# Projections of the delta rule's heads 4 to 7 as nested block products

## The chip, the cores and the metric

The kernel runs on one core of a Trainium2 chip. A core has five engines with a queue of instructions each, worked off in order: TensorE (PE: matmuls, with PEld for loading its stationary operand), VectorE (DVE), ScalarE (ACT), GpSimd (POOL) and SyncE (SP), which here issues the DMAs. They meet through semaphores. Operands lie in SBUF (128 partitions), matmul results in PSUM banks of 128 x 512 floats, everything else in DRAM. The metric is device time in microseconds (us) of one execution.

## The reference, cut to what matters

The kernel computes a layer of 1024 tokens and model width 1024: a feed-forward, a mixer, a second feed-forward, each added to the running x. All is float32.

```python
x = x + 0.5 * swiglu(rms_norm(x), ffn1...)          # gate and up 1024 -> 2816, down 2816 -> 1024
h = rms_norm(x)
proj = h @ w_in                                      # q,k,v | z | b | a | ssm z | ssm x,B,C | dt
q, k, v = silu(causal_dwconv(proj[qkv]))             # 8 heads of 128 channels, 4 taps
o = gated_delta_rule(l2_normalize(q), l2_normalize(k), v, g, beta)
o = rms_norm(o) * silu(proj[z])
y = ssd_scan(...)                                    # 16 state-space heads
x = x + concat([o, y]) @ w_out
x = x + 0.5 * swiglu(rms_norm(x), ffn2...)

# delta rule, chunk by chunk, state S (128 x 128) of each head:
t_inv = inverse(eye + strict_lower(beta * (k @ k.T) * decay))
v_new = t_inv @ (beta * v) - (t_inv @ (beta * exp(gc) * k)) @ S
o     = (q * exp(gc)) @ S + (q @ k.T * decay) @ v_new
S     = S * g_tot + (k * exp(gc_end - gc)).T @ v_new
```

## The kernel before

Every float32 matmul is made of three in a rounded format: both operands are split into a high part (a cast) and a low part (the rest), and hi x hi, lo x hi and hi x lo are summed in one PSUM bank (`mm3`, L120 to 123). Weights are split by `wsplit` (L125 to 138), ScalarE casting (L136) and VectorE subtracting (L137), or by `split2` (L238 to 243). One matmul covers 128 x 128 weights and 512 tokens.

The stages follow one another: first feed-forward (gate and up, then Down), projections and scan of the state-space part (four units), the delta rule (eight heads), the output projection, the second feed-forward.

The feed-forwards and the output use nested block products: a product of matrices cut into 2 x 2 blocks is made of seven block products in place of eight, whose operands are sums and differences of blocks. `a_ops` (L304) makes the weight operands of gate and up on VectorE (sums L315) and ScalarE and VectorE (split, L239 and L240), `prod` (L328) multiplies one. `gate_up_all` calls its inner `prep` (L427) between products, `Down` (L494) has a `prep` (L519) as well; these prepare what later products need.

The input projection is plain. `w_seq` lists the column blocks of w_in, `next_w` hands one out, already split, and prefetches the next into the tile `wst`, with its parts in `whi` and `wlo`. `proj_half` (L757) multiplies 128 columns with 512 tokens of the normalized tokens (`hhi`, `hlo`): 8 blocks x 3 = 24 matmuls, so q, k, v and z of one head take 8 x 24 = 192.

One head of the delta rule (L1112 to 1308):

- q, k, v, z are projected; `conv_silu` (L773) copies the projection into `pre` on ScalarE, multiplies one tap there, and adds three on VectorE (L784). `zc` is the gate, stored to DRAM (L1126).
- k k and q k products of the eight token blocks (L1149, L1150), from which `u` is made.
- The unit lower triangles are inverted. 32 x 32 pieces of `u` go through DRAM (`fs_u`, L1169) and come back as `fu` (L1196), one piece on each partition. Forward substitution takes 31 steps of two VectorE operations, each dependent on the one before it (`ft` L1206, `fx` L1208). The result goes through DRAM again (`fs_x`, L1211, four stores) and comes back by eight small copies into `lv` and `u` (L1218, L1219), all on SP's queue; VectorE transposes `lv` (L1220).
- The solve: small matmuls (L1226 to 1252) put the pieces together, between them copies of ScalarE and VectorE. `kd`, the decayed keys, is scaled out of transposes (L1263, L1265).
- The recurrence over eight blocks (L1269 to 1297), a chain through TensorE and VectorE: k S (L1275), `rr` (L1277), u rr (L1280), `vn` (L1282), k vn (L1289), the new state `sn` (L1294); the output of a block into `vr` by ScalarE (L1297).
- `vr` is normalized (L1303 squares, L1307) and stored to mix_scr.

Work of neighbouring heads overlaps: the substitution of head h runs beside the recurrence of head h - 1, and the projections of head h + 1 fill TensorE between their steps. A scheduler sets each engine's order when the program is built; the queues then run in that order, whatever the times turn out to be. Heads are numbered from 0.

With the last head, `out_start` (L1101) begins the output projection: `group_prep(0)` (L1092) loads rows of w_out into `wst` and makes `mtt` from the state-space outputs. `mtt` lies where hhi and hlo lay.

## Time and profile before

| what | us |
|---|---|
| median of three runs | 2308.49 (2307.07 to 2310.89) |
| the profiled execution, its own time | 2309.97 |
| its span in the trace | 2308.2 |
| TensorE busy | 2272.5 |
| VectorE busy | 1725.1 |
| ScalarE busy | 1088.8 |
| DMA, both ways | 281.42 MB, 122 GB/s on average |

The profile's page gives busy time by engine, the chain of work that ended last, and groups of instructions by line; windows of the trace give the same by stage. A row of a group is: line, engine, operation, written tile <- read tile, shape, count | busy time, mean ns of one | idle time of the engine ahead of it and what ended it. A row of the timeline begins with the start and the duration in us. Matmuls overlap, so that the distance of two starts and not the duration says what one costs. The granted clock is TensorE's, 1.00 at full speed.

### The profile page before, as it was taken

To read this page: it belongs to the slowest core of one execution; us is meant where nothing else is said; L and a number is where in the kernel's file an instruction comes from. 1 tells how busy PE (TensorE), PEld (TensorE's weight loads), DVE (VectorE), ACT (ScalarE), POOL (GpSimd) and SP (SyncE) were. 2 spreads that over 40 slices of the span, in tenths; PEclk is the share of its full clock that TensorE was granted. 3 is DMA by queue.
4 is the path that set the end of the run, shared out by engine and by line. 5 is a ranking of instruction groups with operands and counts; after the bars stand their busy time and mean duration, and the time that the engine had idled before them with its cause. 6 is when DMAs were issued, how large, how long until landed. Compare 5 with 4: busy or idle time off the path is not lost.

```text
span 2308.2 us, 31393 instructions
## 1 busy us (share of the span) xinstructions
PE 2272.5 (98%) x11750; PEld 1858.9 (81%) x11750; DVE 1725.1 (75%) x3349; ACT 1088.8 (47%) x1884; POOL 53.1 (2%) x125
## 2 busy tenths in 40 slices
PE   7999999999999999999999999999999999999998
PEld 5788888888878888878788888788778888888886
DVE  7977776767765675668777888878688777766787
ACT  7433333343367785863555555332543333334344
POOL 0000000000000100000000000000000000000000
PEclk9999999999999999999999999999999999999999
DMA  3333332573652332232333322335223333329446
GB/s 111 127 114 102 105 109 97 178 278 128 222 179 78 92 92 81 67 85 74 83 101 83 82 74 73 104 110 193 79 84 117 109 103 105 109 88 354 139 154 214
DMA packets 231438, 281.42 MB, mean 122 GB/s; under 512 B 57449, under 2 KB 164045, under 8 KB 230261
## 3 DMA queue, kind: packets, MB, share of 16 engines
q1 hardware_dynamic: 231028, 279.31, 37.5%
q8 instruction: 92, 1.51, 0.3%
q14 instruction: 62, 0.50, 0.1%
q0 software_dynamic: 256, 0.10, 0.0%
HBM read 211.59 MB, written 67.77 MB: 121 GB/s over the span
## 4 chain that ended last, share of the span: by engine, by line
PE 87%; DVE 6%; ACT 3%; DMA 2%; issue 1%; SPq 0%; POOL 0%; DVEq 0%; ACTq 0%
PE ps_pj L121 9%; PE ps_pj L123 9%; PE ps_pj L122 9%; PE ps_pj L334 6%; PE ps_pj L332 6%; PE ps_pj L333 6%; PE ps_mx L332 3%; PE ps_mx L334 3%; PE ps_mx L333 3%; PE ps_pj L553 2%; PE ps_pj L554 2%; PE ps_pj L552 2%; PE ps_oo L333 2%; PE ps_oo L332 2%; PE ps_oo L334 2%; PE ps_sc L552 1%
## 5 line engine op out<-in xcount | busy, mean ns | idle before, releaser
L121 PE MATMUL ps_pj<-hhi,whi 128*128 128x512 f32 x832 | 334.3, 402 | 0.4 <-ACT gsb L826 0.4
L123 PE MATMUL ps_pj<-hhi,wlo 128*128 128x512 f32 x832 | 334.5, 402 | 0.0
L122 PE MATMUL ps_pj<-hlo,whi 128*128 128x512 f32 x832 | 331.8, 399 | 0.0
L334 PE MATMUL ps_pj<-bh,al 128*128 128x512 f32 x688 | 267.9, 389 | 0.0
L333 PE MATMUL ps_pj<-bl,ah 128*128 128x512 f32 x688 | 267.8, 389 | 0.0
L332 PE MATMUL ps_pj<-bh,ah 128*128 128x512 f32 x688 | 267.6, 390 | 0.0
L123 PEld LDWEIGHTS ps_pj<-hhi,wlo 128*128 128x128 f32 x832 | 156.7, 188 | 29.6 <-issue 1.9
L122 PEld LDWEIGHTS ps_pj<-hlo,whi 128*128 128x128 f32 x832 | 156.7, 188 | 29.1 <-issue 1.2
L121 PEld LDWEIGHTS ps_pj<-hhi,whi 128*128 128x128 f32 x832 | 156.8, 188 | 28.8 <-ACT gsb L826 0.9
L239 ACT CAST ah<-wst 128x512 fp32r<-128x512 f32 x88 | 54.6, 623 | 223.8 <-PE ps_oo L333 131.4
L239 ACT CAST hid<-hraw 128x1024 fp32r<-128x1024 f32 (+1 forms) x84 | 82.3, 981 | 147.9 <-PE ps_oo L554 62.5
L333 PEld LDWEIGHTS ps_pj<-bl,ah 128*128 128x128 f32 x688 | 129.2, 188 | 26.8
L334 PEld LDWEIGHTS ps_pj<-bh,al 128*128 128x128 f32 x688 | 129.1, 188 | 26.7
L332 PEld LDWEIGHTS ps_pj<-bh,ah 128*128 128x128 f32 x688 | 128.9, 188 | 26.5
L315 DVE TENSOR_TENSOR as<-wst 128x512 f32<-128x512 f32 x220 | 144.8, 683 | 3.3 <-DMA wst<-in_ffn_w_up_dram 3.1
L240 DVE TENSOR_TENSOR al<-as,ah 128x512 fp32r<-128x512 f32 x220 | 140.9, 684 | 4.8 <-ACT ah L239 4.0
L332 PE MATMUL ps_mx<-bh,ah 128*128 128x512 f32 x352 | 138.3, 395 | 4.0 <-ACT m L341 1.4
L333 PE MATMUL ps_mx<-bl,ah 128*128 128x512 f32 x352 | 138.3, 393 | 0.5 <-DVE bl L240 0.5
L334 PE MATMUL ps_mx<-bh,al 128*128 128x512 f32 x352 | 137.7, 391 | 0.3 <-DVE al L240 0.3
L239 ACT CAST ah<-as 128x512 fp32r<-128x512 f32 x220 | 125.0, 618 | 22.6 <-DVE as L315 22.6
L240 DVE TENSOR_TENSOR hid<-hraw,hid 128x1024 fp32r<-128x1024 f32 (+1 forms) x84 | 95.0, 1131 | 34.8 <-ACT hid L239 34.3
L341 ACT COPY m<-ps_pj 128x512 f32<-128x512 f32 x88 | 51.6, 588 | 124.5 <-PE ps_pj L334 122.3
(448 smaller groups left out, 5085.0 us busy)
## 6 DMA issues: line engine op xcount, KB each, us to landing
hraw<-hid_scr SPq DMA_DIRECT2D x70, 512.0 KB, 3.9
hid_scr<-hs SPq DMA_DIRECT2D x110, 256.0 KB, 2.3
wst<-in_ffn_w_down_dram SPq DMA_DIRECT2D x50, 512.0 KB, 4.7
wst<-in_ffn_w_gate_dram SPq DMA_DIRECT2D x22, 1024.0 KB, 5.6
wst<-in_ffn_w_up_dram SPq DMA_DIRECT2D x22, 1024.0 KB, 5.4
wst<-in_w_in_dram SPq DMA_DIRECT2D x36, 512.0 KB, 4.8
hid_scr<-sg SPq DMA_DIRECT2D x44, 256.0 KB, 2.0
keep<-in_ffn_w_down_dram SPq DMA_DIRECT2D x20, 512.0 KB, 5.5
```

The costliest lines, as they stand in the source:

```text
L121: T.matmul(o, lhsT=wh, rhs=mh, start=first, stop=False)
L122: T.matmul(o, lhsT=wh, rhs=ml, start=False, stop=False)
L123: T.matmul(o, lhsT=wl, rhs=mh, start=False, stop=last)
L239: return (A.copy(out=hi, in_=src), V.tensor_tensor(out=lo, in0=src, in1=hi.bitcast(F32), op=ALU.subtract))
L240: V.tensor_tensor(out=lo, in0=src, in1=hi.bitcast(F32), op=ALU.subtract))
L315: V.tensor_tensor(out=t, in0=v[0], in1=v[1], op=v[2])
L332: T.matmul(bank, lhsT=wh[:, k], rhs=bh[:, k], start=a, stop=False, skip_group_check=True)
L333: T.matmul(bank, lhsT=wh[:, k], rhs=bl[:, k], start=False, stop=False, skip_group_check=True)
L334: T.matmul(bank, lhsT=wl[:, k], rhs=bh[:, k], start=False, stop=z, skip_group_check=True)
L341: A.copy(out=t, in_=bank)
L552: T.matmul(bank, lhsT=hh, rhs=wh, start=first and k == 0, stop=False, skip_group_check=True)
L553: T.matmul(bank, lhsT=hh, rhs=wl, start=False, stop=False, skip_group_check=True)
```

## The change

Heads 4 to 7 project q with k, and v with z, by `chunk`: the two column blocks by the two halves of the inner dimension, times the two halves of the inner dimension by the two halves of the tokens. Seven block products of 12 matmuls replace eight of 12. Their weight operands (units) are made during the first feed-forward by `win_units` (six chunks beside gate and up, two beside Down) and stored to DRAM, 7 units of 512 KB for each of 8 chunks; in the delta rule `unit_load` brings them back into four slots, which lie in the tiles of `wst`. The token operands of four of the products are made during the state-space stage by `token_operands`, stored, and loaded once before head 4: three pairs into `natp`'s, `whi`'s and `wlo`'s tiles and into halves of hhi and hlo. In all heads `kd`, `vn` and the scaling of `vr` move from VectorE to ScalarE. `conv_from` takes its first tap from SBUF. `zc` and `qsq` share a tile.

```diff
@@ gate_up_all's prep
+                for _ in range(2 if i % 8 == 7 else 1):
+                    next(side, None)
@@ Down.prep
+            if self.cnt % 2:
+                next(self.side, None)
@@
-    for h in range(GH):
+    for h in range(4):
         w_seq.append((COL_Q + h * P, COL_K + h * P))
         w_seq.append((COL_V + h * P, COL_GZ + h * P))
@@ win_units, for each chunk c
+            raw = raws.tile([P, 2, NK, P], F32, name="wraw")
+            for j, c0 in enumerate(((COL_Q, COL_K), (COL_V, COL_GZ))[c % 2]):
+                nc.sync.dma_start(out=raw[:, j], in_=win_v[:, :, c0 + (c // 2 + NESTED) * P:c0 + (c // 2 + NESTED + 1) * P])
...
+            def unit(m, src):
+                parts = [raws.part(dt) for dt in (F32R, F32R)]
+                split(*parts, src)
+                for i, t in enumerate(parts):
+                    nc.sync.dma_start(out=wu_scr[c][:, IN_ORDER.index(m), i], in_=t.bitcast(F32))
...
+            yield
+            unit(4, a22)
+            s1 = summed(a21, a22, ALU.add)
+            yield
+            unit(5, s1)
...
@@ state-space loop
         proj_z(zts)
+        token_operands(un)
@@
+    def unit_load(s):
+        if s < 7 * len(wu_scr):
+            c, i = divmod(s, 7)
+            u = slots[s % 4]
+            nc.sync.dma_start(out=u.bitcast(F32), in_=wu_scr[c][:, i])
+            units.append((s, u))
+
+    def unit_prod(bank, m, first):
+        s, u = units.pop(0)
+        bh, bl = H_IN[m]
+        for k in range(4):
+            wh, wl = (u[:, i, k * P:(k + 1) * P] for i in range(2))
+            T.matmul(bank, lhsT=wh, rhs=bh[k], start=first and k == 0, stop=False, skip_group_check=True)
+            T.matmul(bank, lhsT=wh, rhs=bl[k], start=False, stop=False, skip_group_check=True)
+            T.matmul(bank, lhsT=wl, rhs=bh[k], start=False, stop=k == 3, skip_group_check=True)
+        unit_load(s + 4)
+
+    def chunk(d0, d1):
+        lo, hi = slice(0, 512), slice(512, L)
+        x = psum("pj")
+        unit_prod(x, 1, True)
+        A.copy(out=d1[:, lo], in_=x)
+        y = psum("pj")
+        unit_prod(y, 6, True)
+        V.tensor_tensor(out=y, in0=y, in1=d1[:, lo], op=ALU.add)
+        A.copy(out=d0[:, hi], in_=y)
+        unit_prod(x, 2, False)
+        A.copy(out=d0[:, lo], in_=x)
+        unit_prod(y, 7, False)
+        z = psum("pj")
+        unit_prod(z, 5, True)
+        A.copy(out=d1[:, hi], in_=z)
+        V.tensor_tensor(out=d1[:, hi], in0=y, in1=d1[:, hi], op=ALU.add)
+        unit_prod(z, 3, False)
+        V.tensor_tensor(out=d0[:, hi], in0=z, in1=d0[:, hi], op=ALU.add)
+        unit_prod(y, 4, False)
+        A.copy(out=d1[:, lo], in_=y)
+
+    def conv_from(pre, c, dst):
+        A.mul(out=dst, in_=pre[:, 3:3 + L], mul=cw_g[:, 3, c:c + 1])
+        conv_taps(pre, cw_g, c, dst)
+        A.activation(out=dst, in_=dst, func=AF.Silu)
@@ delta rule, heads 4 to 7
+                chunk(pre[0][:, 3:3 + L], pre[1][:, 3:3 + L])
+                conv_from(pre[0], h, qt)
+                conv_from(pre[1], 8 + h, kt)
...
+                chunk(pre[:, 3:3 + L], zc)
+                conv_from(pre, 16 + h, vt_)
+                A.activation(out=zc, in_=zc, func=AF.Silu)
@@ all heads
-                V.tensor_tensor(out=kd[:, hb], in0=pt.rearrange("p (i c) -> p i c", i=4),
-                                in1=wend[:, hb, h:h + 1].to_broadcast([P, 4, P]), op=ALU.mult)
+                for i in range(4):
+                    b = half * 4 + i
+                    A.mul(out=kd[:, b], in_=pt[:, i * P:(i + 1) * P], mul=wend[:, b, h:h + 1])
...
-                V.tensor_scalar(out=vn, in0=p2[:, 0:P], scalar1=br2[:, b:b + 1], scalar2=None, op0=ALU.mult)
+                A.mul(out=vn, in_=p2[:, 0:P], mul=br2[:, b:b + 1])
...
-            V.tensor_tensor(out=vr, in0=vr, in1=co.unsqueeze(2).to_broadcast([P, NB, P]), op=ALU.mult)
+            for b in range(NB):
+                A.mul(out=vr[:, b], in_=vr[:, b], mul=co[:, b:b + 1])
```

How it moves instructions. TensorE before, from the last projection matmul of head 7 (L123, `hhi`) to the first solve matmuls of head 6 (L1226, L1227); L1149 and L1150 are head 7's k k and q k products, L121 to L123 with `whi` and `mtt` the output projection:

```order
L123 MATMUL ps_pj_12950<-hhi_4968,wlo_12738 128x512
L1149 MATMUL ps_mx_13018<-kt_12732 128x128
L1150 MATMUL ps_mx_13018<-qt_12731,kt_12732 128x128
...
L121 MATMUL ps_pj_13468<-whi_12987,mtt_12981 128x512
L122 MATMUL ps_pj_13468<-wlo_12988,mtt_12981 128x512
...
L121 MATMUL ps_pj_13492<-whi_12987,mtt_12981 128x512
L1149 MATMUL ps_mx_13048<-kt_12732 128x128
L1150 MATMUL ps_mx_13048<-qt_12731,kt_12732 128x128
L1226 MATMUL ps_sc_12497<-lv_12486,u_12298 32x32
L1227 MATMUL ps_sc_12497<-lv_12486,u_12298 32x32
```

The same place in the changed program (L1225 to L1227 unit products, L1358 and L1359 the k k and q k products, L1435 to L1461 the solve, L1472 kd's transposes, L1489 the recurrence, L123 to L125 output projection):

```order
L1227 MATMUL ps_pj_13488<-hhi_5409,wunits_10680 128x512
L1358 MATMUL ps_mx_13634<-kt_13352 128x128
L1359 MATMUL ps_mx_13634<-qt_13351,kt_13352 128x128
...
L1435 MATMUL ps_sc_13104<-lv_13093,u_12905 32x32
L1436 MATMUL ps_sc_13104<-lv_13093,u_12905 32x32
...
L1444 MATMUL ps_sc_13123<-lv_13093 32x32
...
L1472 MATMUL ps_sc_13184<-ident_183,kt_12659 128x128 x4
L123 MATMUL ps_pj_14082<-whi_13588,mtt_13582 128x512
L124 MATMUL ps_pj_14082<-wlo_13589,mtt_13582 128x512
L1489 MATMUL ps_sc_13193<-vr_12973,u_12905 128x128
```

The output products that stood among head 7's k k products and in front of head 6's solve now begin behind that solve; between the last unit product and the solve stand k k and q k products alone. From the end of the recurrence to the next solve, the count of 128 x 512 projection matmuls was 116 to 123 in front of the solves of heads 4 to 6, and is 130, 113, 82 and 55 in front of those of heads 3, 4, 5 and 6.

SP before, at the same place (w_out's rows, head 5's stored result, head 6's copies from fs_x):

```order
L154 DMA wst_13500<-in_w_out_dram 128x2x1024
L1308 DMA mix_scr2_165<-vr_11662 1024x1x128
L1211 DMA fs_x_12407<-fx_12413 256x1x32 x4
L1218 DMA lv_12486<-fs_x_12407 32x8x32
L1219 DMA u_12298<-fs_x_12407 32x8x32
```

And now, first at head 3's place, where unit loads (L1216) stand between the stores of fs_x and the copies from it, then at head 6's:

```order
L1420 DMA fs_x_10935<-fx_10941 256x1x32 x4
L1216 DMA wunits_10680<-wu_scr2_165 128x1024 x2
L1427 DMA lv_11014<-fs_x_10935 32x8x32
...
L1518 DMA mix_scr2_177<-vr_12280 1024x1x128
L1420 DMA fs_x_13014<-fx_13020 256x1x32 x4
L156 DMA wst_13586<-in_w_out_dram 128x2x1024
L1427 DMA lv_13093<-fs_x_13014 32x8x32
L1428 DMA u_12905<-fs_x_13014 32x8x32
```

A load of weights now stands between fs_x and lv on SP; before, only the four stores were ahead of the copies.

ScalarE in the recurrence of head 5 now (L1491 is vn, L1254 a convolution's tap, L1250 a projection's copy, L1506 and L1512 a block's output and its square):

```order
L1254 ACTIVATE qt_13351<-pre_13354,cols_193 128x1024
L1491 ACTIVATE vn_12565<-ps_sc_12563,br2_12214 128x128
L1506 COPY vr_12280<-ps_oo_12567 128x128
L1512 ACTIVATE jk2_12628,sso_12619<-vr_12280 128x128
L1250 COPY pre2_13355<-ps_pj_13373 128x512
L1254 ACTIVATE kt_13352<-pre2_13355,cols_193 128x1024
L1491 ACTIVATE vn_12581<-ps_sc_12579,br2_12214 128x128
```

Before, vn stood on VectorE among the substitution's operations:

```order
L1277 SCALAR_TENSOR_TENSOR rr_11953<-ps_sc_11951,negeg_5380,vr_11662 128x128
L1208 TENSOR_TENSOR fx_12413<-fx_12413,ft_12414 128x2x24
L1206 TENSOR_TENSOR ft_12414<-fx_12413,fu_12408 128x69
L1208 TENSOR_TENSOR fx_12413<-fx_12413,ft_12414 128x3x23
L1282 TENSOR_SCALAR vn_11957<-ps_sc_11955,br2_11596 128x128
```

The recurrence's chain now passes through ScalarE, and vn can stand behind a 1024-column operation there. On VectorE, 36 of the 62 substitution operations of head 6 stand behind the last rr (L1486) of head 5.

More of the change, by code (lines that the diff above doesn't have):

```diff
@@ L771, in proj_z, with conv_taps @@
                              func=AF.Silu)
+    def conv_taps(pre, cw, c, dst):
+        for t in range(3):
+            V.scalar_tensor_tensor(out=dst, in0=pre[:, t:t + L], scalar=cw[:, t, c:c + 1], in1=dst,
+                                   op0=ALU.mult, op1=ALU.add)
     def conv_silu(pool, w, j, cw, c, dst, bias=None, between=None):
@@ L909, in token_sums, with token_operands, put, step @@
         nc.sync.dma_start(out=dst, in_=scr.rearrange("j (c p) -> p (j c)", p=P))
+    def token_operands(k):
+        b11, b12, b21, b22 = ([hsl(t, k + 4 * i, slice(j * 512, (j + 1) * 512)).bitcast(F32) for t in (hhi, hlo)]
+                              for i in range(2) for j in range(2))
+        def put(m, t):
+            hi = tt.tile([P, 512], F32R, name="thi")
+            lo = tt.tile([P, 512], F32R, name="tlo")
+            split(hi, lo, t)
+            for i, part in enumerate((hi, lo)):
+                nc.sync.dma_start(out=t_scr[m][:, i, k], in_=part.bitcast(F32))
+        def step(t, x, y, op):
+            V.tensor_tensor(out=t, in0=x, in1=y, op=op)
+        t = tt.tile([P, 512], F32, name="tsum")
+        step(t, b22[0], b12[0], ALU.subtract)
+        step(t, t, b22[1], ALU.add)
+        step(t, t, b12[1], ALU.subtract)
+        put(7, t)
+        step(t, t, b11[0], ALU.add)
+        step(t, t, b11[1], ALU.add)
+        put(6, t)
+        step(t, b22[0], t, ALU.subtract)
+        step(t, t, b22[1], ALU.add)
+        put(5, t)
+        for x, y in ((b21[0], b22[0]), (b21[1], b22[1])):
+            step(t, t, y, ALU.subtract)
+            step(t, t, x, ALU.add)
+        put(4, t)
+    tt = cs_.enter_context(tc.tile_pool(name="tokens", bufs=1, side="right", reuse_waits="tile"))
     rstd_g = []
@@ new lines, in first_units, with other_token_tiles @@
+    def first_units():
+        for i in range(2):
+            t = wp.tile([P, 2, 2, 512], F32R, name="wunits", tag="wst")
+            slots.extend(t[:, j] for j in range(2))
+        for s in range(4):
+            unit_load(s)
+    def other_token_tiles():
+        for m, k0, j in ((1, 0, 0), (2, 4, 0), (3, 4, 1), (4, 0, 1)):
+            H_IN[m] = [[hsl(t, k0 + k, slice(j * 512, (j + 1) * 512)) for k in range(4)] for t in (hhi, hlo)]
+        for i, t in enumerate((hhi, hlo)):
+            for j in range(2):
+                nc.sync.dma_start(out=t[j][:, :, 512:L].bitcast(F32), in_=t_scr[4][:, i, 2 * j:2 * j + 2])
+        token_tile(5)
```

102 lines of the change are left out of this document (84 added, 18 removed).

## Prediction

> **What bounds the kernel now.** I read the page's busy shares and its chain first.
>
> ```profile
> PE 2272.5 (98%) x11750; PEld 1858.9 (81%) x11750; DVE 1725.1 (75%) x3349; ACT 1088.8 (47%) x1884; POOL 53.1 (2%) x125
> PE 87%; DVE 6%; ACT 3%; DMA 2%; issue 1%; SPq 0%; POOL 0%; DVEq 0%; ACTq 0%
> L121 PE MATMUL ps_pj<-hhi,whi 128*128 128x512 f32 x832 | 334.3, 402 | 0.4 <-ACT gsb L826 0.4
> ```
>
> TensorE is busy for 98% of the span and 87% of the chain. An average over stages says little of one of them, so I cut the stages that the change touches out of the trace. Columns: window, its length, busy time (instructions) of PE, PEld, DVE, ACT and POOL, granted clock, DMA share, GB/s.
>
> ```profile
> 92.00:460.00 368.00, 367.02 (x1618) 303.30 (x1617) 276.03 (x441) 132.38 (x231) 0.00 (x0) 1.00 0.35 119
> 460.00:520.00 60.00, 60.00 (x266) 49.38 (x265) 40.06 (x41) 29.27 (x35) 0.00 (x0) 1.00 0.76 278
> 760.00:840.00 80.00, 80.00 (x538) 66.60 (x536) 55.30 (x68) 67.48 (x141) 9.30 (x10) 1.00 0.35 103
> 1129.00:1192.00 63.00, 63.00 (x433) 50.99 (x432) 50.49 (x174) 33.40 (x66) 2.46 (x10) 1.00 0.38 101
> 1383.00:1448.00 65.00, 63.68 (x437) 51.69 (x438) 53.12 (x174) 35.20 (x69) 3.28 (x9) 1.00 0.30 90
> ```
>
> They are the first gate and up products, the first Down, one SSM unit, and two periods of the delta rule (one head each). TensorE fills all of them, so a matmul less is time gained wherever the order still finds one to run.
>
> How long is a matmul? The mean of 402 ns is no price: the records overlap. The distance of starts is.
>
> ```profile
> 1413.88 0.39 PE L123 MATMUL ps_pj<-hhi,wlo 128*128 128x512 f32 x1
> 1414.11 0.39 PE L121 MATMUL ps_pj<-hhi,whi 128*128 128x512 f32 x1
> 1414.34 0.39 PE L122 MATMUL ps_pj<-hlo,whi 128*128 128x512 f32 x1
> ```
>
> That is 0.23 us; over the first window it is 367.02/1618 = 0.227. I take 0.2275.
>
> **The change part by part.** *Fewer products.* Eight chunks take 7 x 12 = 84 matmuls in place of 96: 96 fewer, 96 x 0.2275 = **-21.8 us** (by the record's mean it would be 38.6, which the starts rule out).
>
> *Weight operands.* 42 of 56 units are made beside the gate and up products, 14 beside Down. A unit is a cast, a subtraction, mostly a sum, and two stores.
>
> ```profile
> L315 DVE TENSOR_TENSOR as<-wst 128x512 f32<-128x512 f32 x220 | 144.8, 683 | 3.3 <-DMA wst<-in_ffn_w_up_dram 3.1
> L239 ACT CAST ah<-wst 128x512 fp32r<-128x512 f32 x88 | 54.6, 623 | 223.8 <-PE ps_oo L333 131.4
> hid_scr<-hs SPq DMA_DIRECT2D x110, 256.0 KB, 2.3
> ```
>
> VectorE gets 42 subtractions and 30 sums, 72 x 0.683 = 49 us at most, and goes from 276 to 325 of 368; ScalarE from 132 to 158 (42 x 0.623). Writes of 21.5 MB and reads of 6 MB add some 75 GB/s to 119, and the window beside it ran 278 GB/s with TensorE at 60.00 of 60. TensorE's work hides all this; were it late, the 43 us that VectorE has left there are the cover. I take +0.5, bounds 0 and 8 (a sixth of the 49 us in front of a product). Down's 14 units (24 VectorE operations, 7 MB) meet the 0.76 DMA share: +0.5, bounds 0 and 5.
>
> *Token operands.* 44 sums, 16 subtractions and 16 casts over four SSM units: 15 x 0.683 = 10 us of VectorE to a window with 55 of 80 used, 2.5 us of ScalarE to 67 of 80. Hidden by TensorE's 80.00: 0, bounds 0 and 4 (ScalarE has 12 us left).
>
> *VectorE's work moved to ScalarE, all eight heads.*
>
> ```profile
> L1282 DVE TENSOR_SCALAR vn<-ps_sc,br x64: 333/351/352, 1077.5 to 1547.4; 128x128 f32<-128x128 f32 x64
> L1137 ACT ACTIVATE dt<-dt,ngc x64: 384/393/405, 998.2 to 1426.8; 128x128 f32<-128x128 f32 x64
> L136 ACT CAST whi<-wst x64: 1028/1047/1097, 661.6 to 1561.3; 128x1024 fp32r<-128x1024 f32 x64
> L1265 DVE TENSOR_TENSOR kd<-ps_sc,wend x16: 673/675/692, 1075.0 to 1522.9; 128x512 f32<-128x512 f32 x16
> 1393.97 0.35 DVE L1277 SCALAR_TENSOR_TENSOR rr<-ps_sc,negeg,vr 128x128 f32<-128x128 f32 x1 [0.58 <-PE ps_sc L1275]
> 1394.90 0.35 DVE L1282 TENSOR_SCALAR vn<-ps_sc,br 128x128 f32<-128x128 f32 x1 [0.58 <-PE ps_sc L1280]
> 1395.40 0.39 PE L1286 MATMUL ps_oo<-vn,dt 128*128 128x128 f32 x2
> ```
>
> Per head kd, vn and vr's scaling leave VectorE (1.35 + 2.8 + 1.2 us) and become 24 ScalarE operations of about 0.39, so 9 us, onto 33 of 63. The recurrence is a chain with a vn in each of 64 blocks. VectorE waits for TensorE at both of its steps here, and 0.15 us lie between vn's end (1395.25) and its matmul. 0.04 us more per vn hides in that. What doesn't is a wide ScalarE operation (1.05 us) queued ahead of a vn; in the order some ten vn stand right behind a 1024-column one and most behind short ones. The first vn of a head stands behind eight kd, 8 x 0.39 = 3.1 against 1.35, part of it beside the transposes. Bounds 0 and 64 x 0.4 = 26; nearest to the row of vn itself, I take +2 for the wide ones and +1 for kd: **+3**.
>
> *SP's queue.* 56 unit loads of 512 KB come into the delta rule, some right between fs_x and lv (heads 3 to 5), and each waits on SP until its slot is free.
>
> ```profile
> hraw<-hid_scr SPq DMA_DIRECT2D x70, 512.0 KB, 3.9
> lv<-fs_x SPq DMA_DIRECT2D x32, 32.0 KB, 1.9
> fu<-fs_u SPq DMA_DIRECT2D x32, 128.0 KB, 3.0
> wst<-in_w_out_dram SPq DMA_DIRECT2D x8, 1024.0 KB, 5.1
> ```
>
> Each such place can set lv, hence the solve, back by up to one load, 3.9 us. Before the solves of heads 3 to 5 the order holds 130, 113 and 82 projection matmuls behind the recurrence's end (29.6, 25.7, 18.7 us) against some 22 us that the chain needs (next part), so only head 5's lacks cover: **+2**, bounds 0 and 15.
>
> *The hole before head 6's solve.* This is the largest loss. Before, output products were ready by then; now their operands wait for the tiles of the last chunk. The chain there before:
>
> ```profile
> 1412.00 0.42 PE L1280 MATMUL ps_sc<-rr,u 128*128 128x128 f32 x2
> 1412.05 0.23 DVE L1206 TENSOR_TENSOR ft<-fx,fu 128x65 f32<-128x65 f32 x1
> 1412.31 0.23 DVE L1208 TENSOR_TENSOR fx<-fx,ft 128x65 f32<-128x65 f32 x1
> 1430.54 0.17 DVE L1208 TENSOR_TENSOR fx<-fx,ft 128x8 f32<-128x8 f32 x1
> 1430.77 2.56 SPq L1211 DMA_DIRECT2D fs_x<-fx  x4
> 1438.22 0.45 SPq L1219 DMA_DIRECT2D u<-fs_x  x1
> 1442.98 0.44 DVE L1220 STREAM_TRANSPOSE lv<-lv 128x256 f32<-128x256 f32 x1
> 1443.97 0.21 PE L1226 MATMUL ps_sc<-lv,u 32*32 32x32 f32 x1
> 1452.87 0.39 PE L1280 MATMUL ps_sc<-vr,u 128*128 128x128 f32 x2
> ```
>
> From the last fx to the first solve matmul 13.3 us pass, and the last copy would land at 1438.7 + 1.9 = 1440.6, so 11.5 would do; I take 12. In the changed order 36 fx and ft operations stand behind the last rr, with nothing wide between them: 36 x 0.25 + 1 = 10 us. TensorE must so wait until 22 us behind that rr. It has 55 product matmuls (12.5), 16 of q k and k k (128 columns each; half of a 512-column one taken, 0.11: 1.8) and the recurrence's rest (1): 15.3. Hole: **6.7**. From solve to recurrence 8.9 us pass, with six projection matmuls in between before, two now: +1.0; kd on ScalarE there, with nothing beside it, +1.2. Together **+8.9**, bounds 4 (fx at 0.21 each and 11 us behind it, the solve hidden) and 17 (13.3 us from fx to solve as measured, the output weights' load, 5.1 us, late in front of the recurrence, and another 2 us of fx behind wide VectorE work).
>
> *Clock.* A stretch of the trace has a short wait and then slow matmuls.
>
> ```profile
> 1690.00:1700.00 10.00, 8.10 (x29) 5.91 (x28) 9.74 (x17) 4.41 (x8) 0.00 (x0) 0.83 0.67 211
> 1692.99 0.73 PE L332 MATMUL ps_sc<-bh,ah 128*128 128x512 f32 x2 [1.35 <-ACT bh L239]
> 1695.29 0.63 PE L332 MATMUL ps_sc<-bh,ah 128*128 128x512 f32 x1
> 1695.72 0.63 PE L333 MATMUL ps_sc<-bl,ah 128*128 128x512 f32 x1
> 1697.92 0.39 PE L333 MATMUL ps_sc<-bl,ah 128*128 128x512 f32 x1
> ```
>
> Starts 0.43 apart for some seven matmuls, 0.2 lost on each: +1.3 behind the hole, bounds 0 and 5 (the solve's thin stretch as well). The Trainium skill, "TensorE: Matmul & The Clock Gate", section "Why this matters for your kernels", speaks against this change: no idle gap over about 3 us between bursts, since one idle window (about 3.4 us) halves the clock. By it the 6.7 us hole costs a window at half rate, an estimate of 1.7 instead of 1.3; the trace shows the halved rate already behind a wait of 1.35 us.
>
> **Sum.** -21.8 + 0.5 + 0.5 + 3 + 2 + 8.9 + 1.3 = **-5.6** against the profiled execution's 2309.97 (span 2308.2 and 1.8 around it): 2304.4. That execution lies 1.5 above the median 2308.49, so as a median **2302.9**.
>
> **Rivals.** *The hole is covered* (fx runs ahead during the recurrence since VectorE is freed of 5.4 us per head, and output operands come early). For it, between the last rr and fx's end VectorE was the busy one, and it is what is relieved:
>
> ```profile
> 1412.40:1430.70 18.30, 18.30 (x84) 15.06 (x83) 17.83 (x47) 13.86 (x25) 2.44 (x3) 1.00 0.36 116
> ```
>
> 17.83 of 18.30 us. Against: the 36 operations stand behind the last rr in program order. Terms 0.5 + 0.5 + 1 + 1 + 2 remain: -16.8, 2291.7.
>
> *The order slips at every head, and the gain is eaten.* The period falls from 63 to 63 - 24 x 0.2275 = 57.5 us, and one head's chain must fit in it: fu's load 3.0, the 62 fx and ft (15.5 at 0.25 each; 35 x 0.25 and the 18.2 from 1412.31 to 1430.54 are 27, if wide work stands between them as before), 13.3 to the solve, 8.9 behind it: 41 to 52 us. For it: the room falls from 11 to 5.5 at the upper end, and copies through DRAM behind unit loads take 3.9 from it. Against: TensorE showed no wait in these periods. From 5.5 us of new delay per head on it binds; at 7.5, heads 4 to 6 lose 2 each: +6, 2308.9, no change.
>
> *ScalarE makes the recurrence longer* (slower). Place: vn of every block. What is left of the gain, 5.6, with +4.6 needed, is eaten, with the 3 already counted, from 13.2/64 = 0.21 us per block on. For it: in the recurrence of head 5, around its block 4, the queue holds a table load, a Silu of 1024 columns, a square and a copy between two vn. Against: those stretches cover few blocks, and projection matmuls stand between the steps. At 0.25 per block: +16 - 3 - 5.6, 2315.9.
>
> *Unit loads delay the small copies* (slower). Two chains through DRAM (fu, lv) in each of heads 3 to 6 are eight places; at 3.9 us each, less the half that products cover, +16: 2302.9 - 2 + 16 = 2316.9. It decides from 0.8 of a load per head on (12.2 us over four heads). For it: the order has loads ahead of both chains. Against: a load that starts early lands early, and four slots are filled ahead.
>
> A program doing the same products as before is excluded: the order has 96 fewer.
>
> **How the numbers follow.** 0.2%, about what a measurement tells from none, is 4.6 us: faster is under 2303.9, slower over 2313.1. My sum 0.45 (2297 to 2309, of which 0.26 faster, 0.19 same), covered hole 0.20 (faster), slip at every head 0.13 (0.02 faster, 0.09 same, 0.02 slower), ScalarE 0.12 and loads 0.10 (together 0.03 same, 0.19 slower). Faster 0.48, same 0.31, slower 0.21. The range takes the covered case at its near end and the slower ones up to about 2316: 2290 to 2316.
>
> **What would show it.** PE's products 96 fewer at an unchanged 0.2275 us; a gap of TensorE of 4 to 9 us between the last unit product and head 6's solve, released through VectorE's copy of lv, with a clock below 1.00 there; TensorE at 0.98 or more of the gate and up window with VectorE near 320; recurrences no longer than before. Wrong if PE's waits for vn sum to over 10 us, if waits for lv stand at heads 3 to 5, or if no gap stands at head 6.

## The result and the profile after

The changed kernel takes 2323.99 us (median of 4 runs, 2323.72 to 2324.2), the kernel before 2308.34 in the same comparison: ratio 1.0066, 95% interval 1.0049 to 1.0084. Forecast were 2302.9, 2290 to 2316, and faster at 0.48. It is 15.7 us slower. The profiled execution took 2324.2, its span is 2322.5.

Of the page, the busy times and the chain:

```profile
PE 2267.5 (98%) x11654; PEld 1847.8 (80%) x11654; DVE 1776.8 (77%) x3417; ACT 1172.7 (50%) x2124; POOL 51.2 (2%) x125
PE 77%; DVE 10%; ACT 6%; DMA 4%; issue 2%; POOL 0%; SPq 0%; DVEq 0%; ACTq 0%; POOLq 0%
```

The 96 matmuls are gone (11750 to 11654). The chain tells the rest: TensorE's share fell from 87% to 77%, VectorE's, ScalarE's and the DMAs' rose from 11% to 20%. TensorE's own waits (what it waited for: us in total, times, longest):

```profile
PE ps_mx L1358 <- DVE jd L1362: 7.6, 8, 2.4
PE ps_pj L1225 <- DMA wunits<-wu_scr: 3.4, 1, 3.4
PE ps_mx L1358 <- DVE br L1367: 2.0, 1, 2.0
PE ps_mx L334 <- ACT sg L380: 2.0, 1, 2.0
```

In the kernel before, the same products waited 1.6 us in all, and no projection waited for a load:

```profile
PE ps_mx L1149 <- DVE jd L1153: 1.6, 2, 1.3
```

The stages by windows, gate and up, first Down, and then the stretch in front of head 6's solve with the solve itself:

```profile
92.00:460.00 368.00, 366.14 (x1614) 302.57 (x1613) 314.12 (x509) 154.92 (x274) 0.00 (x0) 1.00 0.56 191
460.00:520.00 60.00, 59.52 (x263) 48.94 (x263) 42.00 (x47) 31.05 (x38) 0.00 (x0) 1.00 0.94 335
1423.00:1450.00 27.00, 18.98 (x92) 15.16 (x90) 22.70 (x89) 16.52 (x32) 2.12 (x7) 0.91 0.77 245
1450.00:1463.00 13.00, 12.16 (x139) 9.56 (x140) 7.29 (x25) 6.01 (x14) 0.00 (x0) 0.53 0.37 95
```

Most of the steady gate and up stage is as full as before, with VectorE at 314 (forecast near 320). In front of the solve 8 of 27 us are empty, and the solve runs at a clock of 0.53.

A busy TensorE hides small losses, so I keep a ledger. A stretch between two marks (first gate and up product, first Down product, first projection, first k k product, each solve, each recurrence's first and last L1489, the second feed-forward) has a length, and the order says which matmuls stand in it. At 0.2275 us for 512 columns, in proportion for less (0.028 at least), these are its work; the rest I call lost. Small matmuls cost more than that, so only differences count, and neighbouring stretches are best summed, since the order shifts small matmuls between them. Each column is one profiled execution, up to 3.3 us off its kernel's median (side_held took 2309.2 there against 2312.5, side_all_up 2303.7 against 2307.0), so a difference of a few us between columns can be chance.

| lost, us | before | changed | early_output | moves_undone | early_vector | side_held | side_all_up | side_alone | vn_alone |
|---|---|---|---|---|---|---|---|---|---|
| first gate and up | 11.1 | 13.4 | 14.9 | 13.6 | 14.8 | 11.3 | 11.2 | 16.9 | 11.4 |
| first Down | 3.4 | 5.6 | 3.5 | 4.4 | 4.1 | 6.6 | 2.7 | 4.2 | 3.9 |
| state space | 38.3 | 40.9 | 40.8 | 40.8 | 40.9 | 41.0 | 40.8 | 40.8 | 38.7 |
| eight heads, first solve to last recurrence | 107.9 | 140.9 | 133.3 | 137.6 | 127.4 | 126.4 | 126.7 | 111.2 | 112.2 |
| everything else | 39.2 | 35.3 | 36.6 | 35.1 | 33.5 | 35.7 | 34.2 | 37.7 | 38.3 |
| all | 199.8 | 236.0 | 229.2 | 231.5 | 220.7 | 221.0 | 215.5 | 210.7 | 204.5 |

The work fell by 21.8 us, the losses rose by 36.2, the span by 14.3. Of the 33.0 in the heads, 14.4 lie between the end of head 5's recurrence and the start of head 6's (9.5 in front of the solve, 4.9 in it), 6.4 in front of head 3's solve, 4.2 in front of head 5's, 1.3 in front of head 4's, 7.3 within recurrences; the rest nearly cancels.

### The profile page after: what moved, and what is told of

Read it like the earlier page. It is cut to its first block, busy times and chain, and to the rows that moved or that the text cites. A ratio compares the mean times of both kernels' runs of the same rounds, so it can differ in the third digit from the quotient of the medians.

```text
span 2322.5 us, 32024 instructions
## 1 busy us (share of the span) xinstructions
PE 2267.5 (98%) x11654; PEld 1847.8 (80%) x11654; DVE 1776.8 (77%) x3417; ACT 1172.7 (50%) x2124; POOL 51.2 (2%) x125
## 4 chain that ended last, share of the span: by engine, by line
PE 77%; DVE 10%; ACT 6%; DMA 4%; issue 2%; POOL 0%; SPq 0%; DVEq 0%; ACTq 0%; POOLq 0%
PE ps_pj L123 7%; PE ps_pj L125 7%; PE ps_pj L124 7%; PE ps_pj L334 6%; PE ps_pj L336 6%; PE ps_pj L335 6%; PE ps_mx L334 3%; PE ps_mx L336 3%; PE ps_mx L335 3%; PE ps_oo L336 2%; PE ps_oo L335 2%; PE ps_oo L334 2%; PE ps_pj L560 1%; DMA wst<-in_ffn_w_down_dram 1%; PE ps_pj L561 1%
## 5 line engine op out<-in xcount | busy, mean ns | idle before, releaser
L123 PE MATMUL ps_pj<-hhi,whi 128*128 128x512 f32 x576 | 230.0, 399 | 0.4 <-ACT gsb L895 0.4
L125 PE MATMUL ps_pj<-hhi,wlo 128*128 128x512 f32 x576 | 229.4, 398 | 0.0
L124 PE MATMUL ps_pj<-hlo,whi 128*128 128x512 f32 x576 | 228.9, 397 | 0.0
L123 PEld LDWEIGHTS ps_pj<-hhi,whi 128*128 128x128 f32 x576 | 108.4, 188 | 21.8 <-ACT gsb L895 0.8
L125 PEld LDWEIGHTS ps_pj<-hhi,wlo 128*128 128x128 f32 x576 | 108.4, 188 | 21.5 <-issue 0.9
L124 PEld LDWEIGHTS ps_pj<-hlo,whi 128*128 128x128 f32 x576 | 108.4, 188 | 21.1 <-issue 0.8
L343 ACT COPY m<-ps_pj 128x512 f32<-128x512 f32 x88 | 51.6, 588 | 112.2 <-PE ps_pj L336 109.2
```

The source lines that it names most:

```text
L123: T.matmul(o, lhsT=wh, rhs=mh, start=first, stop=False)
L124: T.matmul(o, lhsT=wh, rhs=ml, start=False, stop=False)
L125: T.matmul(o, lhsT=wl, rhs=mh, start=False, stop=last)
L343: A.copy(out=t, in_=bank)
```

## The experiments

Medians in us; the kernel before ran beside each (2309.9 to 2310.0). Some kernels with thin margins spread widely between executions (early_vector 2306.0 to 2319.6, the changed kernel 2323.7 to 2324.2), so I read medians and intervals.

**act_alone**, the kernel before with the three operations on ScalarE:

```diff
-                V.tensor_tensor(out=kd[:, hb], ...)           # one of 512 columns, twice
+                    A.mul(out=kd[:, b], in_=pt[:, i * P:(i + 1) * P], mul=wend[:, b, h:h + 1])
-                V.tensor_scalar(out=vn, in0=p2[:, 0:P], ...)
+                A.mul(out=vn, in_=p2[:, 0:P], mul=br2[:, b:b + 1])
-            V.tensor_tensor(out=vr, in0=vr, ...)
+                A.mul(out=vr[:, b], in_=vr[:, b], mul=co[:, b:b + 1])
```

> The kernel before, with only kd, vn and the scaling of vr moved to ScalarE. Theory A (ScalarE's place in the chain costs time: the stretches from a recurrence's start to its end lost 7.3 us more in the changed kernel): 5 to 9 us slower than before, 2313 to 2317. Theory B (these stretches lost time to the transfers that run beside them, ScalarE hides): within 2 us of before. VectorE falls by some 40 us either way.

2315.4, ratio 1.0023 (1.0014 to 1.0032). The move costs 5.5 us by itself.

**vn_alone**, the kernel before with only vn moved.

> The kernel before, with vn alone on ScalarE. If vn's place causes the loss of act_alone's recurrences (12 us more than before): recurrences 8 to 12 us more lost than before, the stretches behind them 4 to 9 less, 2313 to 2316. If kd ahead of the first vn causes it: recurrences within 2 us of before, 2309 to 2311.

2314.3, ratio 1.0019 (1.0011 to 1.0028): vn makes most of it. The recurrences lose 12.1 more in the ledger and the stretches behind them 8.1 less, 4.3 net over the heads, for the order also put small matmuls elsewhere. No matmul waits for vn in the trace, but vn is also loaded as a stationary operand, and these loads (PEld) wait longer. First the row of vn, then the loads' waits here and in the kernel before:

```profile
L1282 ACT ACTIVATE vn<-ps_sc,br x64: 347/367/369, 1077.7 to 1550.7; 128x128 f32<-128x128 f32 x64
PEld ps_oo L1286 <- ACT vn L1282: 12.0, 58, 0.4
PEld ps_oo L1286 <- DVE vn L1282: 8.6, 46, 0.3
```

So 4.3 us is the price. The loads' waits grew by 3.4, which is near it, but an idle weight load is not yet an idle matmul, so the path from one to the other is not shown.

**moves_undone**, the changed kernel with all three back on VectorE (the diff above, reversed).

> The changed kernel with kd, vn and the scaling of vr back on VectorE. Theory A: 2315 to 2319, the recurrences lose no more than in the kernel before. Theory B: 2322 to 2326, recurrences as slow as in the changed kernel. A third way: VectorE, 9 us of work per head richer, gets later with the substitution, and the waits in front of the solves grow: 2326 or more.

2320.5, ratio 1.0045 (1.0033 to 1.0058), so some 5 us better than the changed kernel's 1.0066. The total lies between the two theories (A: 2315 to 2319, B: 2322 to 2326), and the place fits neither: the recurrences lose 60.5 where the changed kernel loses 61.6; 3.1 come from the waits in front of the solves.

**side_alone**, the kernel before plus the making and storing of operands that nothing uses. All heads keep their plain projections, no unit or token operand is loaded, and the three operations stay on VectorE. The lines that decide it:

```diff
-    for h in range(4):
+    for h in range(GH):
...
-            if h < NESTED:
+            if True:
...
```

> The kernel before, plus the making and storing of the weight and token operands, which no product uses: heads 4 to 7 are projected plainly, nothing is loaded back, and VectorE keeps its work. Theory A (the side work costs what the first three stages lost): 5 to 9 us slower than before, 2313 to 2317, +2.3 up to Down, +2.2 in Down, +2.6 in the state-space stage. Rival: these losses come from the scheduler's other order alone or the products hide the work as forecast: within 2 us of before.

2320.9, ratio 1.0047 (1.0035 to 1.006): 11 us, more than either expected. Its first gate and up products lose 5.8 more, with a clock of 0.96 in 100 to 140 us.

**side_no_stores**, the same without the stores.

```diff
-                for i, t in enumerate(parts):
-                    nc.sync.dma_start(out=wu_scr[c][:, IN_ORDER.index(m), i], in_=t.bitcast(F32))
```

> side_alone (2320.9; 11.0 over the kernel before) without the 112 stores of units and the 32 of token operands; the operands are still computed, the products still plain, and TensorE's order is the same. Theory A (engine queues: VectorE and ScalarE work stands in front of what products wait for): within 3 us of side_alone, 2318 to 2324. Theory B (28.7 MB more written in the first stages sets back loads): 2311 to 2315, the first stages as in the kernel before.

2321.1, ratio 1.0047 (1.0035 to 1.0059). The writes that are gone are 37.7 MB (105.5 against 67.8 MB written in the two profiles), not the 28.7 of the expectation, and they cost nothing that these two runs can tell. What is left is the work on VectorE and ScalarE, some 8 MB of reads and another order; which of them costs the 11 us, no run separates.

**early_output**, the changed kernel with the output's first operands ahead of head 7's last product.

```diff
+        unit_prod(y, 4, False)
+        A.copy(out=d1[:, lo], in_=y)
+        if between is not None:
+            between()                     # out_early in head 7: w_out rows, nat in natp, mtt in two of hlo's tiles
         unit_prod(z, 3, False)
         V.tensor_tensor(out=d0[:, hi], in0=z, in1=d0[:, hi], op=ALU.add)
-        unit_prod(y, 4, False)
-        A.copy(out=d1[:, lo], in_=y)
```

> The changed kernel with the last two products of each chunk swapped and the output's first operands (w_out rows, mtt, state-space outputs, the last in a tile of natp) prepared ahead of head 7's last product. Output products then stand in front of head 6's solve. Theory A (the wait there is lack of independent matmuls: 14.4 us lost from the end of head 5's recurrence to the start of head 6's): 2310 to 2315. Rival: the chain through SP and VectorE is late itself and the wait only moves to the next solve: 2320 or more.

2316.8, ratio 1.0031 (1.0021 to 1.0042), about 8 us better than the changed kernel, and between the two theories. From head 5's last recurrence block to head 6's first the loss falls from 22.9 to 14.1; before it was 8.5. So 8.8 of the 14.4 us were lack of independent matmuls, since the chain itself got little shorter: from fx to the solve it still took 17.1 us, against 18.5. The half clock shrank with the hole, from 17 us to one stretch of 3.4. The other 5.6 us stayed. The loss in front of head 4's solve rose by 3.7, as the rival had feared for the next solve.

**early_vector**, early_output and moves_undone together.

> moves_undone and early_output together: kd, vn, vr on VectorE, output operands ahead of head 7's last product. If the two losses are apart, 5 and 8 us go: 2311 to 2314. If VectorE's late work is the common cause (jd and br, on which the k k products wait), the gain of the one is lost again: 2316 or more.

2309.7, ratio 1.0003 (0.9993 to 1.0012): the time of the kernel before, and on the fast side of the expected range. The gain over the changed kernel, 14.3, is not clearly more than the two gains added (some 13), for each is known to about 2 us. With the three operations on VectorE the k k products wait less for kt and for jd. The first piece is early_output's, the second early_vector's:

```profile
PE ps_mx L1363 <- ACT kt L1261: 5.3, 2, 3.0
...
PE ps_mx L1363 <- DVE jd L1367: 3.7, 3, 2.2
```

```profile
PE ps_mx L1363 <- ACT kt L1261: 1.9, 1, 1.9
...
PE ps_mx L1363 <- DVE jd L1367: 1.2, 2, 0.9
```

kt's Silu is ScalarE's. In early_output it was late twice. At 1243 us ScalarE itself had waited for VectorE's qt, and at 1308 us the scaling of vr, one of the three operations, stood right ahead of it:

```profile
1240.90 1.06 ACT L1261 ACTIVATE qt<-qt 128x1024 f32<-128x1024 f32 x1 [2.78 <-DVE qt L841]
1305.21 2.43 ACT L1522 ACTIVATE vr<-vr,co 128x128 f32<-128x128 f32 x8
1307.54 1.04 ACT L1261 ACTIVATE kt<-kt 128x1024 f32<-128x1024 f32 x1
```

So VectorE's relief was a loss at that second place. Why the waits for jd fell as well is not shown.

**loads_pool** and **all_three**, unit loads on GpSimd's queue, in the changed kernel and in early_vector.

```diff
-            nc.sync.dma_start(out=u.bitcast(F32), in_=wu_scr[c][:, i])
+            nc.gpsimd.dma_start(out=u.bitcast(F32), in_=wu_scr[c][:, i])
```

> The changed kernel with the 56 unit loads issued by GpSimd instead of SP. Theory A (head 3's missing unit, 3.4 us and half clock behind it, came from a load that stood behind the store of a finished head on SP's queue): no wait for units in front of head 3's solve, 4 to 7 us faster than the changed kernel, 2318 to 2322. Rival (it is the bandwidth: 8 MB of units and token tiles at once): the same wait, 2323 to 2327.

> early_vector with the unit loads on GpSimd's queue. If the three losses are apart: 2306 to 2310, about the time of the kernel before. If the waits in front of the solves come from a chunk's late outputs and not from queues: as early_vector, within 2 us.

2331.5 and 2323.4, ratios 1.0091 (1.007 to 1.0112) and 1.006 (1.0048 to 1.0071): both expectations miss, and loads_pool lies beyond its rival too. Its loss in front of head 3's solve fell from 8.6 to 5.0, yet TensorE still waited there for a unit, though no store stood ahead of the load any more. Elsewhere the small copies came late:

```profile
1235.02 0.47 PE L1225 MATMUL ps_pj<-t,wunits 128*128 128x512 f32 x1 [1.98 <-DMA wunits<-wu_scr]
u<-fs_x SPq DMA_DIRECT2D x32, 32.0 KB, 4.6
PE ps_sc L1435 <- DVE lv L1429: 5.5, 1, 5.5
q0 software_dynamic: 8320, 29.46, 4.3%
```

The copies into u took 1.8 us in the changed kernel and 1.9 before; the wait of 5.5 us stands in front of head 4's solve. The last row says that the edit also put the loads on another kind of queue, which moves 0.10 MB in the changed kernel. So these two runs change the issuing engine, the kind of queue and the times of all loads together, and which of them made the copies late is open.

**late_side**, early_vector with no side work in the first two rounds' code (`if i >= 4:`); **late_side_order**, that with a chunk's products in another order; **vn_on_vector**, late_side with kd and vr on ScalarE.

```diff
-                for _ in range(2 if i % 8 == 7 else 1):
-                    next(side, None)
+                if i >= 4:                                     # late_side
+                    for _ in range(2 if i % 4 == 3 else 1):
+                        next(side, None)
@@
-    IN_ORDER = (1, 6, 2, 7, 5, 4, 3)
+    IN_ORDER = (1, 6, 5, 2, 7, 3, 4)                           # late_side_order, and chunk's lines with it
```

> early_vector (2309.7) with no side work beside the first two rounds of gate and up products, two units in more of the later ones. Theory A (the feed-forward's loss lies in one place, a unit's cast ahead of the first Silu on ScalarE, and half clock behind that wait; beside the steady products the side work is hidden): 2305.5 to 2307.5, the first feed-forward loses 11 to 12 us as in the kernel before, in place of 14.8. Rival (VectorE's added 43 us spread over the stage): 2309 to 2311.

> late_side with a chunk's products in the order 1, 6, 5, 2, 7, 3, 4, so that 24 matmuls and not 12 lie between a product and the next into the same bank, and the first mtt in the other half of hlo. If the waits in front of the solves of heads 3 and 4 (1.4 to 2 us, released by ScalarE's copy of a bank) come from the bank's short cover: 3 to 4 us faster than late_side. Rival: the scheduler now puts 59 projection matmuls in front of head 6's solve, not 91, and the wait there grows by 3 to 7 us: as late_side or slower by up to 4.

> late_side with kd and vr's scaling on ScalarE, vn alone on VectorE. In act_alone the recurrences lost 12 us and the stretches between recurrence and solve gained 9. If vn causes the loss and the freed VectorE the gain: 2 to 6 us faster than late_side. If kd, which also stands ahead of a head's first vn, causes a part of the loss, or the scheduler gives the fill away (65 projection matmuls in front of head 6's solve, 91 in late_side): as late_side or slower by up to 5.

2314.8, 2310.2 and 2323.0; ratios 1.0014 (1.0003 to 1.0025), 1.0008 (0.9999 to 1.0018), 1.0058 (1.0046 to 1.007). late_side tested nothing: the scheduler pulled the cast back to where it had stood, and TensorE waited 2.1 us for the first Silu as ever. The other product order traded losses between stretches (recurrences 56.8, in front of solves 34.4, against 62.5 and 31.7 in late_side); it is the only run here that takes some 6 us out of the recurrences. vn_on_vector is 8 us over late_side and beyond what was expected of it. It has kd and vr on ScalarE, but also 65 matmuls of projections in front of head 6's solve where late_side has 91, so whether kd, vr or the thinner fill costs them is open.

**side_held** and **side_held_order**: the side work tied behind the fourth round's operands.

```diff
+                    if i >= 4:
+                        with tc.issue_after(made[0].ins), tc.issue_after(made[1].ins):
+                            for _ in range(2 if i % 4 == 3 or i == 20 else 1):
+                                next(side, None)
```

> early_vector (2309.7) with the side work tied behind the weight operands of the fourth and later rounds on ScalarE and VectorE, since in late_side the scheduler pulled the first cast forward to where it had stood. Theory A (that cast, 0.6 us and 3.4 us of wait for its load, ahead of the first Silu, is the feed-forward's loss): TensorE's wait for the first Silu falls from 2.3 to about 0.8 us, the stage loses 11 to 12 us in place of 14.8, 2306 to 2308. Rival (VectorE's and ScalarE's added work anywhere in the stage): 2309 to 2311.

> late_side_order (2310.2) with the side work held back as in side_held. The same 2 to 3 us: 2307 to 2308.5. Rival as there: no change.

2312.5 and 2313.8, ratios 1.0011 (1.0002 to 1.002) and 1.0019 (1.0011 to 1.0028): the totals miss, the mechanism at the first Silu holds. ScalarE in the changed kernel, ahead of the first Silu (table load and sg), and TensorE's wait in side_held:

```profile
70.35 0.62 ACT L241 CAST wunit<-wraw 128x512 fp32r<-128x512 f32 x1 [3.30 <-DMA wraw<-in_w_in_dram]
70.88 0.61 ACT L241 CAST ah<-as 128x512 fp32r<-128x512 f32 x1
71.51 1.28 ACT L380 ACT_TABLE_LOAD   x1
```

```profile
PE ps_mx L334 <- ACT sg L380: 0.8, 1, 0.8
```

A cast that waits for its load stood in front, and with it gone the stage loses 11.3, as before (11.1). But Down lost 6.6. At 480 to 500 us the DMA share was 1.03, ScalarE waited 8.6 us for a load of Down's weights, and the cast of hid stood behind it on ScalarE, so hid was 2.1 us late:

```profile
480.00:500.00 20.00, 17.39 (x70) 13.66 (x69) 9.44 (x11) 9.13 (x12) 0.00 (x0) 0.91 1.03 407
493.02 1.05 ACT L241 CAST wd<-keep 128x1024 fp32r<-128x1024 f32 x1 [8.55 <-DMA keep<-in_ffn_w_down_dram]
495.49 0.50 PE L561 MATMUL ps_sc<-wd,hid 128*128 128x512 f32 x1 [2.08 <-ACT hid L241]
```

**side_all_up**, side_held with all units beside gate and up (`UP_CHUNKS = 8`, two in each round).

> side_held (2312.5) with all eight chunks' units made beside gate and up, two at a time from the fourth round on, none beside Down. Theory A (side_held gave its gain back at Down's start, where the DMA engines are busy for the whole of 460 to 500 us and a late unit's cast stands among Down's): Down loses 3.3 to 4.1 us in place of 6.6, the gate and up stage no more than 12, 2306 to 2310. Rival (two units in a round are more than VectorE's room beside a round's products): the gate and up stage loses 15 or more, 2313 or more.

2307.0, ratio 0.999 (0.9981 to 0.9999). Gate and up, and the start of Down:

```profile
92.00:460.00 368.00, 367.01 (x1618) 303.39 (x1617) 324.60 (x529) 164.19 (x287) 0.00 (x0) 1.00 0.64 219
460.00:500.00 40.00, 39.93 (x176) 32.69 (x176) 24.43 (x23) 19.37 (x23) 0.00 (x0) 1.00 0.96 354
```

VectorE at 325 of 368, and TensorE loses nothing: 11.2 and 2.7. The expectation was met. At the median this kernel is 3 us faster than the one before, but the interval only just ends below 1, and 3 us is less than the 0.2% that a forecast could tell.

## Why the prediction was wrong

Two steps failed above all. Where the prediction sets a chain against the matmuls in front of a solve ("the order holds 130, 113 and 82 projection matmuls", "It has 55 product matmuls"), it took each of them as ready when its turn comes; they waited themselves, for a unit at head 3 and for VectorE at heads 5 and 6, and the term of SP's queue came to 11.9 instead of 2. And "12" from fx to the solve, in the hole, was 18.5, so that hole and clock came to 14.4 instead of 10.2. Of the 20 us between the forecast and the result, these two make 14; the recurrences add 4.3 (+7.3, of which 3 were counted), the operands of weights and tokens 6.1, and the rest of the kernel gives some 4 back.

- *Fewer products, -21.8*: right. The work fell by 21.8, at starts 0.23 apart:

```profile
1225.00 0.40 PE L1225 MATMUL ps_pj<-hhi,wunits 128*128 128x512 f32 x1
1225.23 0.39 PE L1226 MATMUL ps_pj<-hlo,wunits 128*128 128x512 f32 x1
1225.46 0.39 PE L1227 MATMUL ps_pj<-hhi,wunits 128*128 128x512 f32 x1
```

- *Weight operands, +0.5 and +0.5*: measured +2.3 and +2.2. "TensorE's work hides all this" holds in the steady stage, as side_all_up shows. It failed at the ends, where I had no row quoted. At the start, one cast waiting for its load ahead of the first Silu costs 1.2 us (TensorE waits 2.0 for sg, 0.8 before and with side_held). In Down the waits that I find are short, 0.5 and 0.4 for wd, and at its end 1.9 for ScalarE's xtb (0.8 before).
- *Token operands, 0*: +2.6, in all kernels that make them, within the bound of 4. Three waits stand there, 0.7 for VectorE's xe, 0.8 for sq and 0.7 for ScalarE's ct, where sq alone took 0.3 before. Both engines had room in the window, but room says nothing of the order within it.
- *ScalarE, +3*: the moves alone cost 5.5, vn alone 4.3 within the heads, and undoing them all gives some 5 back. The size was near; the rival "ScalarE makes the recurrence longer" is true without being the cause of the sign. Of the 7.3 more that the recurrences lose, moves_undone takes back 1.1 and another product order some 6 (late_side_order). What the step did not have is that vr's scaling can stand ahead of another head's Silu on ScalarE; that cost TensorE 2.3 us at one place in early_output, and little in the changed kernel, where TensorE waited 0.5 us for kt. What else lengthened the recurrences is open.
- *SP's queue, +2*: 11.9. The losses in front of the solves of heads 3, 4 and 5 rose by 6.4, 1.3 and 4.2, but in front of none of the three does TensorE wait for the transposed lv. So it was not the loads ahead of the copies that cost this time. What failed is the count of "130, 113 and 82 projection matmuls" as cover, each taken as ready. At head 3 a product waited 3.4 us for its unit, the next eight matmuls started 0.43 apart (1.6 us more), and a k k product waited 0.5 for kt: 5.5 of the 6.4. At head 5 the fill's waits for jd, zc and pre sum to 2.1, at head 4 to 0.6. (The "some 22 us that the chain needs" was head 6's figure as well: at heads 3 and 4 fx alone ended 22.3 and 17.1 us behind the last rr, where 10 was counted, and 18.1 and 20.7 before.) The last product at head 3 that read the unit's slot, a store of SP, the slot's new load, and the product that waited:

```profile
1230.45 0.39 PE L1227 MATMUL ps_pj<-hhi,wunits 128*128 128x512 f32 x1
1230.46 0.57 SPq L1518 DMA_DIRECT2D mix_scr<-vr  x1
1231.13 0.61 SPq L1216 DMA_DIRECT2D wunits<-wu_scr  x1
1236.95 0.76 PE L1225 MATMUL ps_pj<-t,wunits 128*128 128x512 f32 x1 [3.40 <-DMA wunits<-wu_scr]
```

  The slot came free at 1230.84, so the store held the load up by 0.3 us at most. The same wait stands in moves_undone, where that store comes only 6.7 us behind the load, and in loads_pool:

```profile
1228.84 0.32 SPq L1216 DMA_DIRECT2D wunits<-wu_scr  x1
1233.00 0.47 PE L1225 MATMUL ps_pj<-t,wunits 128*128 128x512 f32 x1 [1.47 <-DMA wunits<-wu_scr]
```

  What these have in common is the order of the products. The scheduler put matmuls of the chunk's fifth product ahead of its third and fourth, so that only 12 matmuls, 2.7 us, lie between the last use of a slot and the first use of what is loaded into it, and a unit load takes 4.0 us at the median (5.8 this time, from issue to the product). In early_vector, where the third and fourth stay in front, no product waits for a unit at head 3. So the 130 matmuls counted as cover were the very ones that needed it: I had looked at what a unit load delays, not at how little time it had itself. The rival of the small copies was true in part: lv's landed in 3.1 us at the median, 1.9 before, but at heads 3 to 5 TensorE did not wait for them.
- *The hole, +8.9, and the clock, +1.3*: 14.4 together. The place was right, and so was fx, which ended 9.3 us behind the start of the last rr (10 taken). The failed step is "12" from fx to the solve: it took 18.5, 1431.64 to 1450.16.

```profile
1431.70 4.01 SPq L1420 DMA_DIRECT2D fs_x<-fx  x4
1435.80 1.11 SPq L156 DMA_DIRECT2D wst<-in_w_out_dram  x1
1439.30 0.34 SPq L1427 DMA_DIRECT2D lv<-fs_x  x1
1442.64 0.45 SPq L1428 DMA_DIRECT2D u<-fs_x  x1
```

```profile
1445.31 2.36 DVE L139 TENSOR_TENSOR wlo<-wst,whi 128x1024 fp32r<-128x1024 f32 x2 [0.16 <-ACT whi L138]
1447.85 0.28 DVE L1362 SCALAR_TENSOR_TENSOR jd<-ps_mx,ident 128x128 bf16<-128x128 f32 x1
1449.67 0.44 DVE L1429 STREAM_TRANSPOSE lv<-lv 128x256 f32<-128x256 f32 x1
```

```profile
1448.19 0.79 PE L1358 MATMUL ps_mx<-kt 128*128 128x128 f32 x2 [2.41 <-DVE jd L1362]
```

  The last copy was issued 11.0 us behind fx, 7.5 before. SP's four stores took 4.0 us against 2.6, and the first copy was issued 3.6 us behind them against 1.5, with w_out's load in that gap; that this load slowed the stores' landing is not shown. The last copy landed at 1444.4, yet VectorE transposed lv only at 1449.67: the split of w_out's rows stood ahead of jd there, and jd ahead of the transpose. The prediction's sign had TensorE released through lv; instead it waited for jd (2.2 and 2.4 us), br (2.0) and tk (0.75): the k k products that I counted as fill waited themselves.
- *The clock* I had priced for the hole alone, with the thin solve as a bound of 5. The bound was the case: half the clock for 17 us, through the whole solve.

```profile
1439.00:1445.00 6.00, 1.77 (x14) 1.42 (x13) 5.88 (x19) 4.68 (x6) 0.73 (x5) 1.00 0.78 240
1445.00:1462.00 17.00, 13.16 (x141) 10.06 (x141) 10.43 (x33) 6.54 (x14) 0.00 (x0) 0.50 0.42 128
```

  The Trainium skill, "TensorE: Matmul & The Clock Gate", section "Why this matters for your kernels", has one idle window, behind a gap of over about 3 us, bring half the clock. The trace differs: the longest wait ahead of the half clock was 2.2 us, in a stretch of 6 us in which TensorE was busy for 1.8, and here the measurement decides.
- *The signs*: the 96 fewer matmuls at 0.23, the gap at head 6, the clock below 1.00 and VectorE near 320 (314) with TensorE at 366.1 of 368 came true. The recurrences were to be no longer and lost 7.3 more, and the release was not through lv. Matmuls waited for vn once, for 0.5 us, though the loads of vn as an operand waited 12.8 us in all against 8.6 before.
- *Chances*: the slower cases had 0.21, each as one mechanism. None of them came alone. All cost terms came out above their values at once, 36 against 16.2, and those that had bounds mostly inside them: I had taken each near the low end for a reason of its own, and the queues behind them are the same three. The runs place the recurrences' 7.3 but do not explain them in full.

## What to carry to other kernels

A kernel at 98% TensorE has an order whose every wait is hidden by the fill that you are about to remove; price the change by what each remaining wait has left, for each place, and sum the unhidden ends of all, not the likeliest of each. Work moved to an idle engine lands in front of what the busy one waits for: look for the first and last rounds of a stage, where a cast that waits for a load stands ahead of the chain, and for a product pulled ahead of the load it needs. Count as fill only what is ready: a matmul that waits for a load, or for the engine of the chain, covers nothing. Side work beside the gate and up products cost nothing here once it was held out of the first rounds and of Down, where the DMA share was 1.03.

## What was not expected of the hardware

The copies of 32 KB into u took 1.9 us at the median before, 1.8 in the changed kernel, and 4.6 when unit loads were issued from GpSimd's queue (loads_pool); those into lv took 1.9, 3.1 and 2.9. A stretch of short waits, the longest 2.2 us, was followed by half the clock for 17 us. The DMA engines held 407 GB/s at a share of 1.03 (side_held, 480 to 500 us), where TensorE lost 2.6 of 20 us; at 354 GB/s and 0.96 (side_all_up, 460 to 500 us) it lost nothing.
